# The order of two seven-step products and of the tiles beside them, in one transformer layer on one core

## The chip, the core and the metric

The kernel runs on one core of a Trainium2 chip. The metric is the time of one execution in microseconds (us), as the device gives it; several executions are made, and their median counts. TensorE multiplies, VectorE and ScalarE work on whole tiles of 128 partitions, POOL (GpSimd) and SP (SyncE) mostly issue transfers (DMAs). Each engine takes its own instructions in order and waits for others by semaphores.

## The reference

One decoder layer over 512 tokens of 1,024 channels. What matters here is the first part: a norm, one wide projection, and the two branches that are fed by it.

```python
u = _rmsnorm(h, norm1_g[l])
proj = u @ w_in[l]
a_glu, q, k, v, r, g_low, gate_a, gate_b = _split_cols(proj)

c = a_glu[..., :CONV_CH] * jax.nn.sigmoid(a_glu[..., CONV_CH:])
c = _causal_dwconv(c, conv_dw_w[l], conv_dw_b[l])
...
gk = jax.nn.log_sigmoid((g_low @ w_gate_up[l] + b_gate[l]).astype(jnp.float32)) / GATE_NORMALIZER
...
o = o.reshape(bsz, seq, GLA_VDIM).astype(x.dtype) * jax.nn.silu(r)
```

`v` (values) and `r` (out-gate) are 512 x 1,024 each. The depthwise convolution has 31 taps. Behind this come the attention, the merge, and a feed-forward part, which the change doesn't touch.

## The kernel before

**Splitting.** Every matrix product is made of three float32r products: each operand is split into a high part and a low part (`whi`, `wlo` for a weight), and `mm3` (line 378) adds low x high, high x low and high x high into one bank of PSUM. A weight tile is 128 x 1,024 (512 KB). `split_weight` (line 295) makes the high part with a cast on ScalarE and the low part in one of two ways: by a subtraction on VectorE, or, for the tiles named in `ADDED`, as a negated copy on ScalarE to which POOL adds the weight once more by a transfer (`wlo<-..., accum_op=ALU.add`).

**The order of weights.** `order` (line 168) lists all weight tiles by use. `load` (line 196) issues the transfer of the next of them on SP into one of four `raw` buffers; each split issues one further load. `weight` (line 348) hands out the next tile, sees that two more are split (`LOOK`), and lets `fill` issue a number (`RATES`) of small VectorE jobs from the `chains`: sums of the activations, and the convolution's taps (`conv_tap`). High and low parts have four buffers each. Instructions of one engine are ordered by a planner: it takes whatever is ready, earlier lines first; `issue_after` puts an instruction behind a given one of its engine.

**Seven steps.** `r` and `v` are made by a scheme with seven block products in place of eight (two of them, a11 and a12, are made at the start of the kernel, and a11's result is copied into the banks x by `opened`; five steps are left here: s1, n2, s4, n3, a22; `IN_STEPS`, line 56). Each step has two weight blocks (d = 0, 1) and two row groups (i = 0, 1), 24 matmuls. Weights and activations of a step are sums of quadrants. Those of the activations are made by `form` and `place` (lines 761 and 772) in the chains. Those of the weights are made by transfers that add (POOL): s1 is block (0,0) plus (0,1), in a `kept` tile; n2 is s1 plus (1,1), added in the same tile after s1 is split; s4 is block (1,1) as loaded; n3 is (0,1) plus (1,1); a22 is n2's tile plus (1,0). `load_block` (line 236), `add_n3` and `sum_on` (line 284) issue these.

**Banks.** `Inner` (line 953) runs the steps. n2, n3 and a22 add into the banks x, s1 and s4 into the banks y. After each step `sink` (line 983) takes the result, while the bank goes on adding: before, s1, n2 and a22 are copied on ScalarE, s4 is combined by VectorE from the bank, and n3 is copied by ScalarE to a `tmp` tile and subtracted by VectorE.

**Row layouts.** `w_r` lies in memory in columns. Its blocks are read from `rows_r`, which `lay_rows` (line 99) writes beforehand: eight tiles, two transfers each, from memory to memory, on SP.

**The stage.** After the start come convolution tiles (k = 0 to 4), each a gate tile and a value tile (`glu_gate`, `glu_value`, 24 matmuls each, weights `w_glu` 2k+1 and 2k), with two row layouts beside each of the first four; then all of w_r; the convolution tile 5; then s1 of w_v, the low-rank gate (`low_gate`, 16 matmuls), and the rest of w_v. The decay gate comes in three pieces (`gate`, line 937): small matmuls and absolute values, exponentials, logarithms; `GATE_AT` names the steps after which they are issued. Then the four heads, the first with the queries and keys `w_qk` 0 and 1.

```python
unit = Inner("w_r", sr)
unit.opened("x")
unit.run(IN_STEPS)
for k in range(GLU_AT[0], GLU_AT[0] + GLU_AT[1]):
    glu_gate(k)
    glu_value(k)
unit = Inner("w_v", vt)
unit.opened("x")
unit.run(IN_STEPS[:2])
glow = low_gate()
unit.run(IN_STEPS[2:], gate_at)
```

Of the kernel before, what the change touches and what calls it, by code (L numbers as in the profile page):

```python
# [10 lines left out]
F32 = mybir.dt.float32  # L11
# [31 lines left out]
ET = mybir.EngineType  # L43
ADDED = {("w_glu", 2 * k) for k in (2, 3, 4, 6, 7)} | {("w_qk", m) for m in range(2, KT)}
ADDED |= {(name, m) for name in ("w_gb", "w_gla") for m in range(KT)}
# [33 lines left out]
def trunk_layer(ctx: ExitStack, tc: tile.TileContext, a: dict, out: bass.AP):  # L79
# [113 lines left out]

    loaded = [None]

    def load():
        if len(raws) < len(order):
            name, j = order[len(raws)]
            if name in SEVEN:
                raws.append(load_block(name, *j))  # L200
                return
            raw = None
            if name == "w_up7":
                i, s = j
                name, j = "w_up", {"b": i, "x": FT + i}.get(s)
            if name == "w_r0":
                raw = raw_tile()
                for i in range(2):
                    c = slice((2 * j + i) * P, (2 * j + i + 1) * P)
                    dst = raw[:, i * T : (i + 1) * T].rearrange("p (c x) -> p c x", x=P)  # L210
                    loaded[0] = nc.sync.dma_start(dst, a["w_r"][:4, :, c].rearrange("c p x -> p c x"))
            elif j is not None:
                raw = raw_tile()
                loaded[0] = nc.sync.dma_start(raw, a[name.rstrip("0")][j])
            raws.append(raw)
# [11 lines left out]

    def keep_tile(name):
        if name != "w_down":
            return tp.tile([P, D], F32, tag="x", name=nm("kept"), bufs=3)  # L230
        return fp.tile([P, D], F32, tag="kept", name=nm("kept"), bufs=2)

    INNER = ("w_r", "w_v")
    LOADS = {"a11": (0, 0), "a12": (1, 0), "n2": (1, 1), "n3": (0, 1)}

    def load_block(name, pairs, step, d):

        first = "s1" if name in INNER else "a11"
        if step not in LOADS and step != first:
            return None  # L240
        src = block(name, pairs, d, *LOADS.get(step, (0, 0)))
        n = src.shape[-1]
        if step == first:
            dst = keep_tile(name)[:, :n]
# [10 lines left out]
        if step == "n2":  # L255
            kept[name, pairs, d, "b22"] = dst
        return dst
# [26 lines left out]
    def sum_on(name, pairs, step, d):  # L284

        where = {"a11": (0, 1), "n2": (1, 0)}
        if name in INNER:
            where["s1"] = (1, 1)
            if (step, d) in (("n2", 1), ("s4", 0)):
                add_n3(name, pairs, 0 if step == "n2" else 1)  # L290
        if step in where:
            nxt = block(name, pairs, d, *where[step])
            nc.gpsimd.dma_start(kept[name, pairs, d], nxt, accum_op=ALU.add)

    def split_weight(between=None):
        if len(ready) < len(order):
# [4 lines left out]
            if name in SEVEN or name == "w_up7":  # L301
                raw = operand(name, raw, *spec) if name in SEVEN else up_operand(raw, *spec)
                n = raw.shape[-1]
                if name == "w_up7" and spec[1] == "m":
                    both = wp.tile([P, D], F32R, tag="raw", name=nm("wm"), bufs=4)
                    nc.scalar.copy(both[:, :T], raw)
                    nc.vector.tensor_tensor(both[:, T:], raw, both[:, :T].bitcast(F32), ALU.subtract)
                    ready.append((both[:, :T], both[:, T:]))
                    load()
                    return  # L310
                hi = wp.tile([P, D], F32R, tag="whi", name=nm("whi"), bufs=4)[:, :n]
                lo = wp.tile([P, D], F32R, tag="wlo", name=nm("wlo"), bufs=4)[:, :n]
                nc.scalar.copy(hi, raw)  # L313
                pace[0] = nc.vector.tensor_tensor(lo, raw, hi.bitcast(F32), ALU.subtract)  # L314
# [275 lines left out]

    def sum_tile(i=0, dt=F32):
        if i == 0:
            return sp.tile([P, D], dt, tag="s", name=nm("f"))
        return tp.tile([P, D], dt, tag=("gain", "x")[i - 1], name=nm("sum"), bufs=(1, 3)[i - 1])

# [176 lines left out]
    def place(name, g):  # L772
        if name not in sums1:
            sums1[name] = [sum_tile(i, F32R) for i in {"n2": (1, 2)}.get(name, (0, 0))]
        hi, lo = (x[:, g * T : (g + 1) * T] for x in sums1[name])
        split_by(formed.pop((name, g)), hi, lo)
# [160 lines left out]
    def gate(piece):  # L937
        for h in range(HEADS):
# [10 lines left out]
            else:  # L949
                behind(lambda: nc.scalar.activation(ab[h], ab[h], AF.Ln, bias=1.0))  # L950
                nc.vector.tensor_tensor(ls[h], ls[h], ab[h], ALU.subtract)

    class Inner:
# [10 lines left out]
        def run(self, steps, at=lambda step, i: None):  # L964
            steps = list(steps)
            while steps:
                step, d = steps.pop(0)
                steps.pop(0)
                parts = [(d, weight(self.name, (IN_PAIRS, step, d))) for d in (0, 1)]
                for i in range(2):  # L970
# [3 lines left out]
                    for d, w in parts:  # L974
                        for j in range(2):
# [3 lines left out]
                            mm3(acc, (ah, al), (w[0][:, c], w[1][:, c]), opens, d == 1 and j == 1, step != "s1")  # L979
                    self.sink(step, i, acc)  # L980
                    at(step, i)

        def sink(self, step, i, acc):
            res = self.res
            at = {"n2": (i, 1), "s4": (i, 1), "s1": (2 + i, 1), "n3": (2 + i, 1), "a22": (2 + i, 0), "a12": (i, 0)}
            key = at[step]
            if step in ("a12", "n2", "s1", "a22"):
                res[key] = heap()
                nc.scalar.copy(res[key], acc)
            elif step == "n3":  # L990
                y = tmp()
                nc.scalar.copy(y, acc)
                nc.vector.tensor_tensor(res[key], res[key], y, ALU.subtract)
            else:
                nc.vector.tensor_tensor(res[key], acc, res[key], ALU.subtract)

    def quadrant(step, p):
        k0, k1 = IN_PAIRS[p]
        if step in ("a12", "a22"):
            lo = T // 2 if step == "a22" else 0  # L1000
            return tuple(x[:, lo : lo + T // 2] for x in acts1[k1])
        return tuple(x[:, p * T // 2 : (p + 1) * T // 2] for x in sums1[step])

# [15 lines left out]
    sums_scope.close()  # L1019
# [687 lines left out]
```

## Time and profile before

| what | value |
|---|---|
| runs | 834.89, 833.38, 833.07 us; median 833.38 us |
| the profiled execution | 837.78 us, its span 836.1 us, mean granted clock 0.992 |
| matmuls | 4,090 |
| moved by DMA | 135.60 MB, mean 162 GB/s |

The profile is one execution. A row of the timeline has the start and the duration in us, the engine, the line, the operation, what it writes and reads, how many were merged (x), and in brackets how long the engine had been idle before it and who released it. A row of the windows has the stretch, and for each engine (TensorE, its weight loads, VectorE, ScalarE, POOL) the busy time and the number of instructions; then TensorE's granted clock as a share of full speed, the busy share of the DMA engines, and GB/s. Matmuls overlap, so their own durations (0.39 us) are longer than the distance from one to the next; what counts is the distance. "DMA to landing" is the time from the issue of a transfer to its end: least, median, most. "x4" behind a line's name counts its instructions, and three numbers with slashes are least, median and most in ns. The names `f`, `sum` and `s` are activation sums; in w_r, `f` belongs to s1, s4 and n3 and `sum` to n2.

### The profile page before, as it was taken

The numbers are of one execution on the slowest core, as the hardware profiler recorded it, in microseconds if no ns is written. First come the engines' busy times: TensorE is split into PE (matmuls) and PEld (weight loads), VectorE is DVE, ScalarE is ACT, GpSimd is POOL, SyncE is SP. The second block draws the span as 40 slices with busy tenths as digits, with TensorE's granted clock in tenths as the row PEclk, the third lists the DMA queues.
The fourth block names the chain that finished last, engine by engine and source line by source line (L and its number), as shares of the span: only waits on it lengthen the run. The fifth ranks groups of instructions, "written<-read, shape, count | busy, mean of one in ns | idle before, by whom it ended". The sixth has DMA issues, their size and how long they took to land.

```text
span 836.1 us, 11021 instructions
## 1 busy us (share of the span) xinstructions
PE 819.6 (98%) x4090; PEld 694.7 (83%) x4090; DVE 677.2 (81%) x996; ACT 471.5 (56%) x671; POOL 116.8 (14%) x139
## 2 busy tenths in 40 slices
PE   9999899999999999999999999999999999999996
PEld 7888688788888888888888898888789888988885
DVE  6899598899999889854678768769957788588896
ACT  7673346795534553359445559655446643577554
POOL 2001202011211221000001012111112012220111
PEclk9999899999999999999999999999999999999999
DMA  9499878658666677321346639456825737556562
GB/s 316 149 271 295 156 217 184 170 154 211 143 147 151 151 175 186 119 100 51 126 99 194 175 137 227 102 126 151 223 92 151 176 77 226 151 152 192 137 125 101
DMA packets 49925, 135.60 MB, mean 162 GB/s; under 512 B 4592, under 2 KB 17152, under 8 KB 49872
## 3 DMA queue, kind: packets, MB, share of 16 engines
q1 hardware_dynamic: 37456, 90.91, 30.9%
q0 software_dynamic: 12240, 43.78, 29.4%
q8 instruction: 32, 0.52, 0.2%
q10 hardware_dynamic: 176, 0.20, 0.1%
q14 instruction: 21, 0.17, 0.1%
HBM read 132.79 MB, written 6.29 MB: 166 GB/s over the span
## 4 chain that ended last, share of the span: by engine, by line
PE 79%; DVE 8%; DMA 7%; ACT 3%; issue 2%; POOL 0%; POOLq 0%; ACTq 0%; DVEq 0%; SPq 0%
PE mm L383 22%; PE mm L384 22%; PE mm L382 22%; PE ax L382 2%; PE mm L652 2%; PE ax L383 2%; PE ax L384 2%; DMA kept<-in_w_o_dram 2%; DVE c L799 2%; DMA kept<-in_w_v_dram 1%; DMA raw<-rows 1%; DVE wlo L314 1%; DVE wlo L339 1%; DMA kept<-rows 1%; PE ax L1125 1%
## 5 line engine op out<-in xcount | busy, mean ns | idle before, releaser
L382 PE MATMUL mm<-uh,wlo 128*128 128x512 f32 (+1 forms) x636 | 237.1, 373 | 0.0
L383 PE MATMUL mm<-ul,whi 128*128 128x512 f32 (+1 forms) x636 | 234.9, 369 | 0.6 <-DVE ul L473 0.6
L384 PE MATMUL mm<-uh,whi 128*128 128x512 f32 (+1 forms) x636 | 234.4, 369 | 0.0
L799 DVE SCALAR_TENSOR_TENSOR c<-h,pp,c 128x507 f32<-128x507 f32 (+21 forms) x240 | 169.7, 731 | 2.9
L384 PEld LDWEIGHTS mm<-uh,whi 128*128 128x128 f32 x636 | 119.8, 188 | 20.4
L383 PEld LDWEIGHTS mm<-ul,whi 128*128 128x128 f32 x636 | 120.0, 189 | 19.2 <-DVE ul L473 1.1
L382 PEld LDWEIGHTS mm<-uh,wlo 128*128 128x128 f32 x636 | 119.9, 189 | 18.3
L330 ACT CAST whi<-raw 128x1024 fp32r<-128x1024 f32 x94 | 97.4, 1042 | 35.2 <-PE mm L384 28.5
L332 ACT ACTIVATE wlo<-raw 128x1024 fp32r<-128x1024 f32 x45 | 47.5, 1059 | 74.2 <-PE mm L382 72.4
L313 ACT CAST whi<-raw 128x1024 fp32r<-128x1024 f32 (+1 forms) x53 | 53.9, 1027 | 49.9 <-PE mm L384 36.4
L313 ACT CAST whi<-kept 128x1024 fp32r<-128x1024 f32 (+1 forms) x44 | 44.3, 1010 | 54.9 <-DMA kept<-rows 16.8
L1366 DVE SCALAR_TENSOR_TENSOR tmp<-mm,pp,tmp 128x511 f32<-128x511 f32 (+1 forms) x88 | 64.5, 742 | 12.6 <-ACT tmp L1364 12.2
L314 DVE TENSOR_TENSOR wlo<-raw,whi 128x1024 fp32r<-128x1024 f32 (+1 forms) x53 | 65.7, 1248 | 9.0 <-ACT whi L313 8.5
L339 DVE TENSOR_TENSOR wlo<-raw,whi 128x1024 fp32r<-128x1024 f32 x49 | 59.3, 1219 | 13.0 <-ACT whi L330 12.6
L314 DVE TENSOR_TENSOR wlo<-kept,whi 128x1024 fp32r<-128x1024 f32 (+1 forms) x44 | 51.3, 1172 | 20.4 <-ACT whi L313 20.2
L1364 ACT ACTIVATE tmp<-mm,pp 128x512 f32<-128x512 f32 x44 | 33.3, 775 | 11.6 <-PE mm L384 11.6
L1286 DVE TENSOR_TENSOR hres<-hres,mm 128x512 f32<-128x512 f32 (+1 forms) x49 | 32.4, 670 | 2.4 <-PE mm L384 2.3
L333 POOL DMA_DIRECT2D wlo<-in_w_up_dram x18 | 15.5, 862 | 95.6 <-ACT wlo L332 77.7
L383 PE MATMUL mm<-wlo,sh 128*128 128x512 f32 x66 | 25.9, 393 | 0.0
L384 PE MATMUL mm<-whi,sh 128*128 128x512 f32 x66 | 25.7, 389 | 0.0
L382 PE MATMUL mm<-h,wlo 128*128 128x512 f32 x64 | 25.4, 397 | 0.0
L382 PE MATMUL mm<-whi,sl 128*128 128x512 f32 x66 | 25.1, 391 | 0.2 <-ACT whi L313 0.2
(362 smaller groups left out, 1645.3 us busy)
## 6 DMA issues: line engine op xcount, KB each, us to landing
raw<-in_w_up_dram SPq DMA_DIRECT2D x44, 512.0 KB, 4.2
wlo<-in_w_up_dram POOLq DMA_DIRECT2D x18, 512.0 KB, 7.5
raw<-in_w_glu_dram SPq DMA_DIRECT2D x16, 512.0 KB, 4.5
raw<-in_w_down_dram SPq DMA_DIRECT2D x15, 512.0 KB, 5.0
kept<-in_w_down_dram POOLq DMA_DIRECT2D x10, 512.0 KB, 5.2
raw<-in_w_v_dram SPq DMA_DIRECT2D x8, 512.0 KB, 6.5
rows<-in_w_r_dram SPq DMA_DIRECT2D x16, 256.0 KB, 7.2
raw<-in_w_qk_dram SPq DMA_DIRECT2D x8, 512.0 KB, 6.0
```

The source lines that it names most:

```text
L313: nc.scalar.copy(hi, raw)
L314: pace[0] = nc.vector.tensor_tensor(lo, raw, hi.bitcast(F32), ALU.subtract)
L330: nc.scalar.copy(hi, raw)
L332: pace[0] = nc.scalar.activation(lo, raw, AF.Copy, scale=-1.0)
L339: pace[0] = nc.vector.tensor_tensor(lo, raw, hi.bitcast(F32), ALU.subtract)
L382: nc.tensor.matmul(acc, ll, rh, start=first, stop=False, **kw)
L383: nc.tensor.matmul(acc, lh, rl, start=False, stop=False, **kw)
L384: nc.tensor.matmul(acc, lh, rh, start=False, stop=last, **kw)
L799: nc.vector.scalar_tensor_tensor(y[:, s:], c[:, : T - s], w, y[:, s:], ALU.mult, ALU.add)
L1286: nc.vector.tensor_tensor(hres[t, n][:, c], hres[t, n][:, c], x[:, c], op)
L1364: nc.scalar.activation(z, acc, AF.Identity, bias=pp[:, PP_FB + m : PP_FB + m + 1], scale=w[2])
L1366: nc.vector.scalar_tensor_tensor(z[:, s:], acc[:, : T - s], w[j], z[:, s:], ALU.mult, ALU.add)
```

## The change

- The steps run in the order s1, s4, n2, n3, a22. The s4 block (1,1) is the one that is loaded; n2 is split without a load of its own, and such steps no longer use up a load (`skipped`, and `load` calls itself).
- Four convolution tiles come before w_r. The tiles 4 and 5 are put into w_r and w_v: the gate tile behind s1 (in w_v behind the low-rank gate), the value tile behind n3. The banks x are opened after the gate tile.
- s1, s4 and a22 are copied by ScalarE; n2 and n3 are subtracted by VectorE straight from the bank.
- All 16 row layouts are issued beside the tiles 0 and 1, after the first and after the second `w_glu` load.
- `w_qk` 0 and 1 get their low parts by adding transfers. Three of the four subtractions of the log decays go to POOL.
- In `Inner` the taps are issued after each half step, behind its `sink`, no longer before its matmuls. The sums of n2 go to four convolution buffers; the second `kept` tile of w_v goes to the buffer `gain`, the first has a third `x` buffer.
- The decay gate's pieces come after s4, n2 and n3 of w_v (i = 1 each).

```diff
-ADDED = {("w_glu", 2 * k) for k in (2, 3, 4, 6, 7)} | {("w_qk", m) for m in range(2, KT)}
+ADDED = {("w_glu", 2 * k) for k in (2, 3, 4, 6, 7)} | {("w_qk", m) for m in range(0, KT)}
-IN_STEPS = [(step, d) for step in ("s1", "n2", "s4", "n3", "a22") for d in (0, 1)]
-GLU_AT = (5, 1, 2)
+IN_STEPS = [(step, d) for step in ("s1", "s4", "n2", "n3", "a22") for d in (0, 1)]
+GLU_AT = (4, 2, 2)
-GATE_AT = [("n2", 0), ("s4", 0), ("n3", 1)]
+GATE_AT = [("s4", 1), ("n2", 1), ("n3", 1)]
...
-    order += [("w_r", (IN_PAIRS, step, d)) for step, d in IN_STEPS]
-    order += [("w_glu", 2 * k + j) for k in range(GLU_AT[0], late) for j in (1, 0)]
-    v_steps = [("w_v", (IN_PAIRS, step, d)) for step, d in IN_STEPS]
-    order += v_steps[:2] + [("w_low", 0), ("w_low", 1)] + v_steps[2:]
+    for i, name in enumerate(("w_r", "w_v")):
+        for step, d in IN_STEPS:
+            order.append((name, (IN_PAIRS, step, d)))
+            if (step, d) == ("s1", 1):
+                order += [("w_low", 0), ("w_low", 1)] if name == "w_v" else []
+                order.append(("w_glu", 2 * (GLU_AT[0] + i) + 1))
+            if (step, d) == ("n3", 1):
+                order.append(("w_glu", 2 * (GLU_AT[0] + i)))
...
                 raws.append(load_block(name, *j))
+                if name in INNER and raws[-1] is None:
+                    load()
                 return
...
-                loaded[0] = nc.sync.dma_start(raw, a[name.rstrip("0")][j])
+                sent[name, j] = nc.sync.dma_start(raw, a[name.rstrip("0")][j])
...
-    def keep_tile(name):
+    def keep_tile(name, d):
+        if name == "w_v" and d == 1:
+            return tp.tile([P, D], F32, tag="gain", name=nm("kept"), bufs=1)
...
+    IN_LOADS = {"s1": (0, 0), "s4": (1, 1), "n3": (0, 1)}
...
-            if (step, d) in (("n2", 1), ("s4", 0)):
-                add_n3(name, pairs, 0 if step == "n2" else 1)
+            if (step, d) in (("s4", 0), ("s4", 1)):
+                add_n3(name, pairs, d)
...
+                skipped = name in INNER and raws[len(ready)] is None
                 ready.append((hi, lo))
-                load()
+                if not skipped:
+                    load()
...
-    def weight(name, j, ahead=LOOK):
+    def weight(name, j, ahead=LOOK, taps=True):
...
-        fill(RATES.get(name if name != "w_glu" or j < 2 * (KT - GLU_AT[2]) else "late", RATE))
+        if taps:
+            fill(RATES.get(name if name != "w_glu" or j < 2 * (KT - GLU_AT[2]) else "late", RATE))
...
+        if name == "n2":
+            sums1[name, g] = [ctile(F32R) for _ in range(2)]
...
-        for n in ("s1", "n2", "s4", "n3"):
+        for n in ("s1", "s4", "n2", "n3"):
             chain += [(1, lambda n=n, g=g: place(n, g)) for g in range(2)]
...
-        for j in range(2 * k, min(2 * k + 2, KT)):
-            with tc.issue_after(loaded[0].ins):
-                lay_rows(j)
+        if k < 2:
+            for j in ((0, 4, 1, 5), (6, 7, 2, 3))[k]:
+                with tc.issue_after(sent["w_glu", 1 - k].ins):
+                    lay_rows(j)
...
-                nc.vector.tensor_tensor(ls[h], ls[h], ab[h], ALU.subtract)
+                (nc.gpsimd if h >= 1 else nc.vector).tensor_tensor(ls[h], ls[h], ab[h], ALU.subtract)
...
-                parts = [(d, weight(self.name, (IN_PAIRS, step, d))) for d in (0, 1)]
+                parts = [(d, weight(self.name, (IN_PAIRS, step, d), taps=False)) for d in (0, 1)]
...
                     self.sink(step, i, acc)
+                    fill(RATES[self.name])
...
-            if step in ("a12", "n2", "s1", "a22"):
+            if step in ("a12", "s4", "s1", "a22"):
                 res[key] = heap()
                 nc.scalar.copy(res[key], acc)
-            elif step == "n3":
-                y = tmp()
-                nc.scalar.copy(y, acc)
-                nc.vector.tensor_tensor(res[key], res[key], y, ALU.subtract)
             else:
-                nc.vector.tensor_tensor(res[key], acc, res[key], ALU.subtract)
+                nc.vector.tensor_tensor(res[key], res[key], acc, ALU.subtract)
...
-    unit = Inner("w_r", sr)
-    unit.opened("x")
-    unit.run(IN_STEPS)
-    for k in range(GLU_AT[0], GLU_AT[0] + GLU_AT[1]):
-        glu_gate(k)
-        glu_value(k)
-    unit = Inner("w_v", vt)
-    unit.opened("x")
-    unit.run(IN_STEPS[:2])
-    glow = low_gate()
-    unit.run(IN_STEPS[2:], gate_at)
+    for i, (name, res) in enumerate((("w_r", sr), ("w_v", vt))):
+        unit = Inner(name, res)
+        unit.run(IN_STEPS[:2])
+        if name == "w_v":
+            glow = low_gate()
+        glu_gate(GLU_AT[0] + i)
+        unit.opened("x")
+        at = gate_at if name == "w_v" else lambda step, i: None
+        unit.run(IN_STEPS[2:8], at)
+        glu_value(GLU_AT[0] + i)
+        unit.run(IN_STEPS[8:], at)
```

More of the change, by code (lines that the diff above doesn't have):

```diff
@@ L192, in trunk_layer @@
     pace = [None]
-    loaded = [None]
+    sent = {}
     def load():
@@ L210, in load @@
                     dst = raw[:, i * T : (i + 1) * T].rearrange("p (c x) -> p c x", x=P)
-                    loaded[0] = nc.sync.dma_start(dst, a["w_r"][:4, :, c].rearrange("c p x -> p c x"))
+                    nc.sync.dma_start(dst, a["w_r"][:4, :, c].rearrange("c p x -> p c x"))
             elif j is not None:
                 raw = raw_tile()
-                loaded[0] = nc.sync.dma_start(raw, a[name.rstrip("0")][j])
+                sent[name, j] = nc.sync.dma_start(raw, a[name.rstrip("0")][j])
             raws.append(raw)
@@ L234, in trunk_layer @@
     LOADS = {"a11": (0, 0), "a12": (1, 0), "n2": (1, 1), "n3": (0, 1)}
+    IN_LOADS = {"s1": (0, 0), "s4": (1, 1), "n3": (0, 1)}
     def load_block(name, pairs, step, d):
         first = "s1" if name in INNER else "a11"
-        if step not in LOADS and step != first:
+        loads = IN_LOADS if name in INNER else LOADS
+        if step not in loads:
             return None
-        src = block(name, pairs, d, *LOADS.get(step, (0, 0)))
+        src = block(name, pairs, d, *loads[step])
         n = src.shape[-1]
         if step == first:
-            dst = keep_tile(name)[:, :n]
+            dst = keep_tile(name, d)[:, :n]
             kept[name, pairs, d] = dst
@@ L254, in load_block @@
                 add_n3(name, pairs, d)
-        if step == "n2":
+        if step == ("s4" if name in INNER else "n2"):
             kept[name, pairs, d, "b22"] = dst
@@ L589, in trunk_layer, with sum_tile @@
     sums_scope, sp = scoped("sums", 6, "right")
[L591 to L594, printed above, removed]
+    def sum_tile(dt=F32):
+        return sp.tile([P, D], dt, tag="s", name=nm("f"))
     whole = {}
@@ L772, in place @@
     def place(name, g):
[L773 to L776, printed above, removed]
+        if name == "n2":
+            sums1[name, g] = [ctile(F32R) for _ in range(2)]
+        elif g == 0:
+            both = [sum_tile(F32R) for _ in range(2)]
+            for n in range(2):
+                sums1[name, n] = [x[:, n * T : (n + 1) * T] for x in both]
+        split_by(formed.pop((name, g)), *sums1[name, g])
     def sums_chain():
@@ L1001, in quadrant @@
             return tuple(x[:, lo : lo + T // 2] for x in acts1[k1])
-        return tuple(x[:, p * T // 2 : (p + 1) * T // 2] for x in sums1[step])
+        return tuple(x[:, p % 2 * T // 2 : (p % 2 + 1) * T // 2] for x in sums1[step, p // 2])
     def gate_at(step, i):
```

## The prediction

> **What bounds the kernel now.** I read the page first, then the busy time by stretches, then the order of TensorE's matmuls around the two gaps, and last what the other engines and queues did there.
>
> ```profile
> span 836.1 us, 11021 instructions
> PE 819.6 (98%) x4090; PEld 694.7 (83%) x4090; DVE 677.2 (81%) x996; ACT 471.5 (56%) x671; POOL 116.8 (14%) x139
> ...
> 100.00:105.00 5.00, 4.59 (x11) 3.63 (x12) 5.00 (x7) 2.10 (x4) 0.85 (x1) 0.50 1.00 179
> ...
> 160.00:165.00 5.00, 2.95 (x10) 2.02 (x9) 3.37 (x6) 4.99 (x9) 0.00 (x0) 0.81 0.02 5
> ...
> 170.00:420.00 250.00, 250.00 (x1169) 209.01 (x1168) 208.33 (x333) 136.23 (x193) 30.48 (x33) 1.00 0.55 143
> ```
>
> TensorE is the bound: busy 98% of the span, and 250 of 250 us behind the changed stage. VectorE has 208 of those 250, so an earlier start of TensorE is passed on to the end. Only its idle time and its slow clock can be won, and in the stage that the diff touches there are two such places: 94 to 105 us, and 160 to 166 us, each with idle time and a granted clock of 0.5 to 0.8 behind it.
>
> ```profile
> 88.78 0.39 PE L382 MATMUL mm<-whi,f 128*128 128x512 f32 x1
> ...
> 94.00 0.39 PE L384 MATMUL mm<-whi,f 128*128 128x512 f32 x1
> ...
> 106.57 0.39 PE L382 MATMUL mm<-whi,f 128*128 128x512 f32 x1
> ...
> 160.16 0.39 PE L384 MATMUL mm<-whi,f 128*128 128x512 f32 x1
> 162.60 0.50 PE L382 MATMUL mm<-whi,ul 128*128 128x512 f32 x1 [2.05 <-ACT tmp L992]
> ...
> 169.80 0.39 PE L382 MATMUL mm<-uh,wlo 128*128 128x512 f32 x1
> ```
>
> The first two rows are the first and the last of the 24 matmuls of step s1 of w_r: (94.00 - 88.78) / 23 = 0.227 us from start to start. A step of 24 is 5.45 us, a convolution tile (48) 10.9.
> - Step n2 of w_r could start at 94.23 and step s4 starts at 106.57: 12.34 us for 5.45 of work, a loss of **6.89**.
> - Step a22 of w_v could start at 160.39 and the first query starts at 169.80: 9.41 for 5.45, a loss of **3.96**, of which 162.60 - 160.39 = 2.21 is the gap and 1.75 the slow clock behind it.
>
> ```profile
> 76.30 1.23 DVE L314 TENSOR_TENSOR wlo<-kept,whi 128x1024 fp32r<-128x1024 f32 x1 [1.68 <-ACT whi L313]
> ...
> 81.94 1.22 DVE L314 TENSOR_TENSOR wlo<-kept,whi 128x1024 fp32r<-128x1024 f32 x1
> ...
> 84.73 0.87 POOL L260 DMA_DIRECT2D raw<-rows  x1 [12.57 <-DVE c L799]
> ...
> 86.54 1.18 POOL L293 DMA_DIRECT2D kept<-rows  x1
> 90.36 0.87 POOL L293 DMA_DIRECT2D kept<-rows  x1 [2.65 <-issue]
> ...
> 95.03 1.04 ACT L313 CAST whi<-kept 128x1024 fp32r<-128x1024 f32 x1 [10.40 <-DMA kept<-rows]
> 97.60 1.05 ACT L313 CAST whi<-kept 128x1024 fp32r<-128x1024 f32 x1 [1.53 <-DMA kept<-rows]
> ...
> 159.11 1.28 ACT L950 ACT_TABLE_LOAD   x1
> 160.41 1.67 ACT L950 ACTIVATE tmp<-tmp 128x512 f32<-128x512 f32 x3
> 161.98 0.56 ACT L992 COPY tmp<-mm 128x512 f32<-128x512 f32 x1
> ```
>
> The first loss: n2's weights are s1's with one more block added by a transfer, which may start only when s1's low part is made (77.5 and 83.2). The transfers are issued at 86.54 and 90.36, since POOL's queue first sat 12.57 us in front of another add, and ScalarE can cast their results at 95.03 and 97.60. The second: the copy of n3's result (L992), which a22 needs gone from its bank, stands behind a table load and three logarithms on ScalarE.
>
> **The change, part by part.**
>
> *Reordering w_r and w_v* (s1, a gate tile, s4, n2, n3, a value tile, a22). Matmuls, transfers and their sizes stay the same in number. Between s1 and n2 there are now a tile of 5.45 and s4 of 5.45: n2 starts 16.35 after s1's start instead of 5.45. Once issued, the two adds needed 95.03 - 86.54 = 8.5 and 97.60 - 90.36 = 7.2. That fits, so the 6.89 goes. In w_v, n3 is subtracted by VectorE straight from the bank, with no copy on ScalarE, and the value tile gives it 5.45 before a22: the 3.96 goes. Together **-10.85**. What is late next follows.
>
> *The value tile of w_r* takes w_glu 8, which is in ADDED both before and after (its low part is a negated copy plus an adding transfer). In the plain run of tiles its buffers came free two tiles, 10.9 us, ahead of use. Now four whi buffers reach back to n2's first half, whose last use is the 18th of 24 matmuls: 6 x 0.227 + 5.45 (n3) = 6.8 us.
>
> ```profile
> 55.89 1.06 ACT L332 ACTIVATE wlo<-raw 128x1024 fp32r<-128x1024 f32 x1 [1.23 <-PE mm L382]
> ...
> 57.26 0.87 POOL L333 DMA_DIRECT2D wlo<-in_w_glu_dram  x1 [9.62 <-ACT wlo L332]
> ...
> DMA to landing us min/median/max: 3.6/5.7/13.5
> ...
> DMA to landing us min/median/max: 5.1/7.0/12.0
> ...
> 562.20 0.38 PE L382 MATMUL ax<-n,wlo 128*128 128x256 f32 x1 [1.56 <-ACT mm L1554]
> ...
> 562.30:566.00 3.70, 3.70 (x28) 3.57 (x29) 3.67 (x7) 2.39 (x4) 0.00 (x0) 1.00 0.73 267
> ```
>
> High part 1.04 (as the cast at 95.03), low part 1.06, then 57.26 - 56.95 = 0.31 to the issue: 2.4. The two lines of landings are those of the adds into kept (L293) and into wlo (L333). With 3.6 the chain is 6.0 and nothing waits; with 5.7 it is 8.1, 1.3 late; with 7.0 it is 9.4, 2.6 late; with 12.0, 7.6 late. I take 5.7, as L293's adds are the ones in this stage: **+1.3**. A gap of 1.56 at 562 us left the clock at 1.00, so I add no slow clock.
>
> By the Trainium skill (TensorE: Matmul & The Clock Gate, "HAM oscillation") only gaps over about 3.4 us throttle TensorE. The gap of 2.05 at 160 us was followed by a granted clock of 0.81, so here the measurement decides; by the rule a gap of 2.6 would cost 1.75 less than I charge for it below.
>
> *n2 and n3 now follow each other in the same two banks*; before, s4 lay between. n3's first half may start when VectorE has taken n2's first half, 2.72 us after its end. The nearest rows are s4's subtractions.
>
> ```profile
> 110.69 0.68 DVE L995 TENSOR_TENSOR h<-mm,h 128x512 f32<-128x512 f32 x1
> ...
> 154.66 1.28 DVE L995 TENSOR_TENSOR h<-mm,h 128x512 f32<-128x512 f32 x2
> ...
> L946 DVE TENSOR_SCALAR h<-ax,pp x3: 740/740/750, 148.5 to 149.8; 128x512 f32<-128x512 f32 x3
> ```
>
> In w_r: s4's first half ended at 106.57 + 2.72 = 109.29 and was taken at 111.37, 0.64 before the limit. In w_v: s4 ran from 160.39 - 10.9 = 149.49, its first half ended at 152.21 and was taken at 155.34, 3.13 later, 0.4 past the limit. I take **+0.4**; the bounds are 0 and, if two splits (1.22 each) and four gate operations (0.74) go ahead in VectorE's queue, 5.4 + 0.68 - 2.72 = 3.4.
>
> *First query and key by adding transfers*: two VectorE operations of 1.22 go, two of 1.06 on ScalarE, two POOL issues and 2 x 512 KB come. The query's buffers come free with n3's end, and the value tile and a22 cover 10.9; the chain is 2.4 + 7.0 = 9.4: 0. Without the cover: were the table load and logarithms (1.28 + 4 x 0.56 = 3.5) to stand ahead, it is 2.0 late. Three subtractions of the log decays move from VectorE to POOL; the key's add may queue behind them, but the heads that need them come a head later. 0, at most one such wait of 2.0.
>
> *Row layouts earlier*: all 16 issues are moved up SP's queue, from behind the eighth and the tenth convolution load to behind the first (8) and the second (8).
>
> ```profile
> 19.06 24.94 SPq L214 DMA_DIRECT2D raw<-in_w_glu_dram  x8
> 44.05 8.05 SPq L105 DMA_DIRECT2D rows<-in_w_r_dram  x8
> ...
> 25.00:30.00 5.00, 5.00 (x24) 4.14 (x23) 3.80 (x5) 3.84 (x5) 0.00 (x0) 1.00 0.43 150
> ...
> DMA to landing us min/median/max: 3.1/4.2/6.9
> ...
> 31.71 2.35 DVE L339 TENSOR_TENSOR wlo<-raw,whi 128x1024 fp32r<-128x1024 f32 x2
> ...
> 38.58 1.29 DVE L556 TENSOR_TENSOR ul<-f,uh 128x512 fp32r<-128x512 f32 x2
> ...
> 39.47 0.40 PE L382 MATMUL mm<-uh,wlo 128*128 128x256 f32 x2
> ...
> 41.28 2.36 DVE L339 TENSOR_TENSOR wlo<-raw,whi 128x1024 fp32r<-128x1024 f32 x2
> ...
> L105 SPq DMA_DIRECT2D rows<-in_w_r_dram x16: 564/728/2736, 44.1 to 65.6; - x16
> ...
> DMA to landing us min/median/max: 5.6/7.2/9.4
> ```
>
> The DMA engines are at 0.43 there, so there is room. Behind eight issues (8.05) the second load leaves at 19.4 + 8.05 = 27.4; at the median 4.2 (the first line of landings) it lands at 31.6 and is split by 33.9, before the 34.06 at which its low part was ready: 0, with 2.55 as the upper bound (first rival below). The taps' new place, the sums in other buffers and w_v's kept tile in the gain buffer hide behind TensorE's matmuls: 0.
>
> **Sum**: -10.85 + 1.3 + 0.4 = **-9.15**. The profiled execution took 837.78 (span 836.1 and 1.7 around it), so 828.6; it is 4.4 above the median of the runs, 833.38, and I carry that over: **824.2**.
>
> **The rivals.**
> 1. *The second convolution load lands late.* At 6.9 it lands at 34.3, is split at 36.6 instead of 34.06, and VectorE does everything behind it 2.55 later. TensorE has nothing to give there: its matmuls at 39.5 follow the low parts that VectorE ends at 39.87 with no slack. Loss 2.55 + 1.75 of slow clock: 828.5. Against it: the share of 0.43. By the Trainium skill (DMA: Bandwidth & Descriptors, "Queues, rings and completion order") each DMA engine takes a ring's descriptors in order, which speaks for it.
> 2. *The add into w_glu 8 takes the 7.0 of the other wlo adds*: 2.6 idle, long enough for the slow clock (the gap of 2.05 was), 1.75: 824.2 + 3.05 = 827.3.
> 3. *The change doesn't remove the first loss.* From low part to cast it was 95.03 - 77.53 = 17.5 in all, queueing included. If s1's second weight is split only just before use (1.36 into s1), 16.35 - 1.36 - 2.3 = 12.7 are there: 4.8 late, + 1.75: 830.7. Against it: the adds that held POOL's queue now come after s4's splits.
> 4. *Slower: the layouts crowd out the convolution loads.* Before, 16 layouts with their company took from 44.05 to 65.6 + 9.4 (the last line), 31 us. Taking that from 19.4, the second load lands half way, at 34.9 (split at 37.2, 3.1 late), and w_glu 3, behind all of them, at 50.4 (split at 52.7, where the second tile starts at 88.78 - 4 x 10.9 = 45.2: 7.5 late). With two slow clocks 14.1: 824.2 + 14.1 = 838.3. It decides once w_glu 3 lands after about 45.4. For it: SP's order is free to put all 16 first. Against it: blocks of w_r and convolution tiles were loaded in those 31 us as well.
>
> **How the numbers follow.** Forecast 0.45 (its own range 822.5, with no new wait, to 826), rival 1 0.13, rival 2 0.20, rival 3 0.12, rival 4 0.10. The range 821.8 to 831.5 holds all but rival 4 and the long ends of the rest. A measurement of this kernel can tell some 0.2%, 1.7 us: faster 0.85, within 0.06 (ends of rivals 3 and 4), slower 0.09.
>
> **What would show it.** Right: no idle time of TensorE before n2 of w_r and a22 of w_v, clock 1.0 there, the casts of kept no longer waiting for a transfer; about 1 us of idle before the value tile of w_r, put down to the add into wlo; n3's first matmul waiting at most half a us for VectorE. Wrong: TensorE idle between 33 and 46 us, or over 2 us before that value tile or the first query.

## The result, and the profile after

The kernel after the change took 829.45 us (median of 4 runs, 828.47 to 830.39), the kernel before 833.89 on the same chip (833.07 to 834.89): a ratio of 0.9939, interval 0.9914 to 0.9964, or 4.4 us less. The profiled execution took 828.47 against 837.78.

The page of the profile after (span and engines), two stretches around the place of the first loss, and TensorE's two longest kinds of wait (line waited at, what ended the wait, total us, times, longest):

```profile
span 826.8 us, 11023 instructions
PE 813.3 (98%) x4090; PEld 689.9 (83%) x4090; DVE 676.8 (82%) x991; ACT 471.0 (57%) x669; POOL 123.1 (15%) x144
...
100.00:105.00 5.00, 4.70 (x21) 3.57 (x19) 4.94 (x8) 1.98 (x3) 0.04 (x1) 1.00 0.91 202
105.00:110.00 5.00, 3.62 (x16) 3.00 (x17) 5.00 (x8) 0.78 (x1) 0.00 (x0) 1.00 0.06 17
...
PE mm L395 <- DMA wlo<-in_w_glu_dram: 1.9, 2, 1.7
PE mm L395 <- DMA wlo<-in_w_qk_dram: 1.6, 1, 1.6
```

The two old losses are no longer there: n2 follows without a wait, TensorE is busy 5.00 of 5.00 us from 155 to 160, where w_v's a22 now runs, and the clock is 1.00 in both stretches. Two new waits are there, each for a low part made by an adding transfer. ScalarE's low part of w_glu 8 and POOL's issue of its add, then TensorE's matmuls around the two waits:

```profile
97.71 1.06 ACT L344 ACTIVATE wlo<-raw 128x1024 fp32r<-128x1024 f32 x1 [1.80 <-PE mm L396]
...
99.18 0.87 POOL L345 DMA_DIRECT2D wlo<-in_w_glu_dram  x1 [6.67 <-ACT wlo L344]
...
104.31 0.39 PE L397 MATMUL mm<-whi,f 128*128 128x512 f32 x1
106.38 0.50 PE L395 MATMUL mm<-uh,wlo 128*128 128x512 f32 x1 [1.69 <-DMA wlo<-in_w_glu_dram]
...
181.58 0.39 PE L397 MATMUL mm<-uh,whi 128*128 128x512 f32 x1
183.56 0.50 PE L395 MATMUL mm<-uh,wlo 128*128 128x512 f32 x1 [1.60 <-DMA wlo<-in_w_qk_dram]
```

The first is w_r's value tile, waiting for the add into w_glu 8: 106.38 - 104.31 - 0.23 = 1.84 lost. The second is the second head's query, waiting for w_qk 2: 1.75 lost. So of the two profiled executions: -6.89 - 3.96 + 1.84 + 1.75 = -7.26. The remaining 2.05 of the 9.31 lies outside the changed stage. Some 1.0 of it comes ahead of the stage (the matmul that starts at 33.72 before starts at 32.69), and most of the rest is the wait of 1.56 at 562 us, which the prediction quotes and which has no counterpart in this execution.

POOL's adds into a block of n3 (`raw`) and into s1's tiles (`kept`), and the first of n2's casts, which had waited for a transfer before:

```profile
71.01 0.85 POOL L270 DMA_DIRECT2D raw<-rows  x1 [5.30 <-DMA raw<-rows]
71.67 1.10 POOL L303 DMA_DIRECT2D kept<-rows  x1
74.22 0.86 POOL L303 DMA_DIRECT2D kept<-rows  x1 [1.45 <-DVE c L813]
...
84.13 1.05 ACT L323 CAST whi<-kept 128x1024 fp32r<-128x1024 f32 x1
```

The adds leave at 71.67 and 74.22 instead of 86.54 and 90.36; the casts at 84.13 and 88.91 wait for no transfer. That agrees with the reordering, but the adds' *issue* is 15 to 16 us earlier. Most of that is w_r's own start, a tile earlier (s1's first matmul comes at 77.34 instead of 88.78); a longer way from s1 to n2 gives none of the rest. It made me doubt the cause.

### The profile page after: what moved, and what is told of

Its sections match the earlier page's. It is cut to its first block, busy times and chain, and to the rows that moved or that the text cites. A ratio compares the mean times of both kernels' runs of the same rounds, so it can differ in the third digit from the quotient of the medians.

```text
span 826.8 us, 11023 instructions
## 1 busy us (share of the span) xinstructions
PE 813.3 (98%) x4090; PEld 689.9 (83%) x4090; DVE 676.8 (82%) x991; ACT 471.0 (57%) x669; POOL 123.1 (15%) x144
## 4 chain that ended last, share of the span: by engine, by line
PE 78%; DVE 11%; DMA 4%; issue 3%; ACT 2%; POOL 1%; SPq 0%; POOLq 0%; ACTq 0%; DVEq 0%
PE mm L396 22%; PE mm L395 22%; PE mm L397 22%; DVE c L813 4%; PE ax L395 2%; DMA wlo<-in_w_glu_dram 2%; PE mm L663 2%; PE ax L396 2%; PE ax L397 2%; DVE wlo L324 1%; DMA kept<-rows 1%; DMA x<-in_x_dram 1%; PE ax L1137 1%; DVE tmp L1378 1%; PE ax L474 0%
## 5 line engine op out<-in xcount | busy, mean ns | idle before, releaser
L813 DVE SCALAR_TENSOR_TENSOR c<-h,pp,c 128x507 f32<-128x507 f32 (+20 forms) x240 | 169.9, 733 | 2.8
L344 ACT ACTIVATE wlo<-raw 128x1024 fp32r<-128x1024 f32 x47 | 49.5, 1058 | 69.6 <-PE mm L395 65.5
L351 DVE TENSOR_TENSOR wlo<-raw,whi 128x1024 fp32r<-128x1024 f32 x47 | 56.9, 1220 | 16.7 <-ACT whi L342 16.3
```

The lines of the kernel that those rows point to most:

```text
L344: pace[0] = nc.scalar.activation(lo, raw, AF.Copy, scale=-1.0)
L813: nc.vector.scalar_tensor_tensor(y[:, s:], c[:, : T - s], w, y[:, s:], ALU.mult, ALU.add)
```

## The experiments

A median here is of the kernel's runs beside runs of the kernel before on the same chip; those of one group share chip and runs.

**First group: the edits priced at nothing and the new wait** (before: 834.6 us).

*The kernel after again, unchanged.*

> The changed kernel once more. Theory A (the profiled execution of the kernel before was an unusually long one, the changed kernel's was an ordinary one): the profile again shows the waits of TensorE for the adds into w_glu 8 and w_qk 2 at 1.5 to 2.5 us each, no loss before n2 and a22, total 828 to 830 us. Theory B (the changed kernel has new waits that come in some executions only): the profile shows losses of 2 us or more at other places, and the total moves by more than 2 us from 829.5.

831.68 us (12 runs, 828.72 to 835.36), ratio 0.9968 (0.9952 to 0.9984). This profiled execution took 834.58. Its matmuls at the value tile, then two stretches (the last three numbers are the clock, the DMA share and GB/s):

```profile
108.93 0.80 PE L395 MATMUL mm<-uh,wlo 128*128 128x512 f32 x1 [3.58 <-DMA wlo<-in_w_glu_dram]
...
105.00:110.00 5.00, 1.43 (x5) 0.88 (x4) 5.00 (x8) 1.13 (x2) 0.00 (x0) 0.77 0.26 70
110.00:115.00 5.00, 5.00 (x14) 3.92 (x13) 1.19 (x2) 0.00 (x0) 0.00 (x0) 0.54 0.00 0
```

The wait for w_glu 8 is 3.58 here, with a slow clock behind it: the prediction's second rival, in another execution of the same kernel. Neither theory holds whole: the places of the waits are A's, the size of this one and the total are B's.

*w_glu 8's low part by VectorE instead of the adding transfer.*

```diff
-ADDED = {("w_glu", 2 * k) for k in (2, 3, 4, 6, 7)} | {("w_qk", m) for m in range(0, KT)}
+ADDED = {("w_glu", 2 * k) for k in (2, 3, 6, 7)} | {("w_qk", m) for m in range(0, KT)}
```

> The low part of w_glu 8 is made by VectorE again, all else as in the changed kernel. If the wait before the value tile of w_r (1.96 us in the profile) is the add's chain of 2.4 us plus the transfer against the 6.8 us that the buffers leave, it goes and the kernel is 1.5 to 2 us shorter, about 827.5 us. Rival: VectorE, 5.0 of 5.0 us busy there, takes 1.2 us more and is late with the next subtraction from the banks or the next split: no gain, or under 0.5 us.

829.01 us (6 runs), 0.994 (0.9922 to 0.9957): 2.7 less than the kernel after in the same group. The wait at the value tile is gone, the one for w_qk 2 (1.4) stays. By the medians the add's price is 2.7 us on this chip, wait and clock together; the size is rough, since the intervals of the two kernels just meet.

*All log-decay subtractions on VectorE, as before.*

```diff
-                (nc.gpsimd if h >= 1 else nc.vector).tensor_tensor(ls[h], ls[h], ab[h], ALU.subtract)
+                nc.vector.tensor_tensor(ls[h], ls[h], ab[h], ALU.subtract)
```

> All four subtractions of the log decays on VectorE, all else as in the changed kernel. Theory: the three on POOL (1.56 us each) slow VectorE's operations beside them (1.79 and 2.32 us where 0.68 and 1.22 are usual), so VectorE gains nothing; without them the first head's scan comes at most 1 us later or earlier, the operations of VectorE go back to 0.68 and 1.22 us, and the wait for the add into w_qk 2 (1.9 us) shrinks by 0 to 1.5 us. Rival: VectorE has 2.05 us more to do, the scan is 2 us later, and the wait grows to 3 to 4 us.

831.7 us (12 runs), 0.9976 (0.9961 to 0.9991): the same as the kernel after, so no worth of the move to POOL can be seen. What it does to VectorE is told at the end.

*First query and key's low parts by VectorE, as before.*

```diff
-ADDED = {("w_glu", 2 * k) for k in (2, 3, 4, 6, 7)} | {("w_qk", m) for m in range(0, KT)}
+ADDED = {("w_glu", 2 * k) for k in (2, 3, 4, 6, 7)} | {("w_qk", m) for m in range(2, KT)}
```

> The first query's and key's low parts by VectorE again, all else as in the changed kernel. My prediction put this edit at 0: within 0.7 us of the changed kernel. Rival: VectorE, which has no idle time there, gets two operations of 1.2 us more, the first head's scan and with it ScalarE's exponentials and the low part of w_qk 2 come 2 us later, and TensorE's wait there grows from 1.9 to about 4 us.

831.67 us (12 runs), 0.9971 (0.9953 to 0.9989): the edit costs and brings nothing that can be seen. TensorE's one long wait at the first query in this kernel:

```profile
160.80 0.50 PE L395 MATMUL mm<-uh,wlo 128*128 128x512 f32 x1 [1.19 <-DVE wlo L351]
```

With two more splits VectorE is late at the first query instead, while the wait at w_qk 2 goes: one wait is exchanged for another.

**Second group: which part removes the losses** (before: 834.37 us).

*The kernel before again, unchanged.*

> The kernel before once more, with a profile of its own. Theory A: this execution is an ordinary one near 834 us; the loss before n2 of w_r is smaller than the 6.89 us of the first profile, or has no slow clock behind it, and the mean granted clock is above 0.992; the two losses add up to some 6 to 7 us. Theory B: the two losses are again 10.5 to 11 us and the profile is about 838 us, so that profiling itself adds some 4 us to this kernel and none to the changed one.

833.41 us (12 runs), 0.9992 (0.9976 to 1.0008); profiled execution 832.54. Around the first loss, then the stretch of the second, and ScalarE ahead of it; below, the row of the first profile of before in which the second of these casts stands:

```profile
93.03 0.39 PE L384 MATMUL mm<-whi,f 128*128 128x512 f32 x1
94.32 0.50 PE L382 MATMUL mm<-whi,sum 128*128 128x512 f32 x1 [0.90 <-ACT whi L313]
95.58 0.50 PE L383 MATMUL mm<-wlo,sum 128*128 128x512 f32 x1 [0.76 <-DVE wlo L314]
98.38 0.49 PE L382 MATMUL mm<-whi,sum 128*128 128x512 f32 x1 [1.39 <-ACT whi L313]
99.64 0.50 PE L383 MATMUL mm<-wlo,sum 128*128 128x512 f32 x1 [0.77 <-DVE wlo L314]
...
105.24 0.39 PE L382 MATMUL mm<-whi,f 128*128 128x512 f32 x1
...
155.00:170.00 15.00, 15.00 (x68) 12.40 (x67) 14.26 (x22) 13.12 (x19) 0.00 (x0) 1.00 0.30 103
...
153.39 1.99 ACT L313 CAST whi<-kept 128x1024 fp32r<-128x1024 f32 x2
```

```profile
158.04 1.05 ACT L313 CAST whi<-kept 128x1024 fp32r<-128x1024 f32 x1 [2.32 <-DMA kept<-in_w_v_dram]
```

The first loss is there again: 105.24 - 93.26 - 5.45 = 6.53. The second is not: TensorE is busy 15.00 of 15.00 us at clock 1.00. In the first profile the cast at 158.04 had waited 2.32 us for a late transfer, and the table load, the logarithms and the copy behind it were late with it. Here both casts are done by 155.38. This is theory A.

*The kernel before with the early row layouts alone.*

```diff
-        for j in range(2 * k, min(2 * k + 2, KT)):
-            with tc.issue_after(loaded[0].ins):
-                lay_rows(j)
+        if k < 2:
+            for j in ((0, 4, 1, 5), (6, 7, 2, 3))[k]:
+                with tc.issue_after(sent["w_glu", 1 - k].ins):
+                    lay_rows(j)
```

> The kernel before with the row layouts alone moved up to the first two convolution tiles, the order of the steps as before. If the first loss came from the late layouts (POOL's queue stood 12.6 us in front of an add whose block had not landed), n2's weights are ready when s1 ends and most of the first loss goes: 3 to 6 us shorter than before. Rival (mine in the prediction): the order of the steps is what does it; the adds still take 7 to 8.5 us from issue against a step of 5.45 us, so at most half of the loss goes, 0 to 3 us.

826.51 us (6 runs), 0.9918 (0.989 to 0.9947). SP's queue and POOL's, one low part of s1, the first cast of n2, and two stretches; below them SP's row of before for the same loads, and the same two stretches of the kernel before, run again:

```profile
19.44 3.40 SPq L105 DMA_DIRECT2D rows<-in_w_r_dram  x3
...
55.80 13.28 SPq L249 DMA_DIRECT2D raw<-rows  x4
...
74.53 1.22 DVE L315 TENSOR_TENSOR wlo<-kept,whi 128x1024 fp32r<-128x1024 f32 x1
...
76.62 0.86 POOL L261 DMA_DIRECT2D raw<-rows  x1 [5.11 <-issue]
77.22 1.18 POOL L294 DMA_DIRECT2D kept<-rows  x1
81.78 0.87 POOL L294 DMA_DIRECT2D kept<-rows  x1 [3.38 <-DVE wlo L315]
...
84.61 1.05 ACT L314 CAST whi<-kept 128x1024 fp32r<-128x1024 f32 x1
...
20.00:45.00 25.00, 25.00 (x162) 22.70 (x161) 20.67 (x29) 17.20 (x24) 1.45 (x2) 1.00 1.00 307
...
90.00:110.00 20.00, 20.00 (x90) 16.57 (x89) 17.88 (x23) 9.72 (x13) 0.86 (x1) 1.00 0.66 178
```

```profile
71.27 2.86 SPq L248 DMA_DIRECT2D raw<-rows  x4
```

```profile
20.00:45.00 25.00, 25.00 (x163) 22.69 (x162) 21.13 (x30) 17.46 (x25) 1.02 (x2) 1.00 0.47 159
...
90.00:110.00 20.00, 16.19 (x61) 12.12 (x60) 14.76 (x19) 8.59 (x11) 1.73 (x2) 0.91 0.80 182
```

With s1 and n2 still side by side, TensorE is busy 20.00 of 20.00 us. The layouts leave from 19.44 on, into DMA engines that had been at 0.47; the blocks laid out by rows are asked for from 55.80 instead of 71.27. In the kernel before, a block that was asked for from 71.27 on took a median of 11.0 us to land, which fits the add into n3's block that POOL could issue only at 84.73, though that row names a VectorE operation. Here the like add leaves at 76.62 after 5.11 us of standing, and s1's adds behind it at 77.22 and 81.78, 1.5 and 0.4 us after their low parts are made (75.75 and 81.38). The first cast of n2 is 10.4 us earlier (84.61 against 95.03). This part alone removes the first loss. The gain of 7.9 us is above the 3 to 6 that I expected; the two profiled executions, 825.77 here and 832.54 of the kernel before run again, differ by 6.77, near the loss of 6.53.

*The kernel after with the row layouts late, as before.*

```diff
-        if k < 2:
-            for j in ((0, 4, 1, 5), (6, 7, 2, 3))[k]:
-                with tc.issue_after(sent["w_glu", 1 - k].ins):
-                    lay_rows(j)
+        for j in ((0, 4), (1, 5), (6, 7), (2, 3))[k]:
+            with tc.issue_after(loaded[0].ins):
+                lay_rows(j)
```

> The changed kernel with the row layouts issued beside the first four convolution tiles as before (two each, in the new order of tiles). Mine: the order of the steps gives n2 16.3 us behind s1's start, so n2 still doesn't wait; but w_r starts a tile earlier, and its first blocks come 10 us later than in the changed kernel, so s1 may wait: 0 to 4 us longer than the changed kernel. Rival: the early layouts are what removed the loss: 5 us or more longer, near the time before.

837.06 us (8 runs), 1.0036 (1.0021 to 1.0051): longer than before by 2.7 us, as the rival says. The rows of POOL, ScalarE and VectorE, and among them TensorE's first matmul of n2 (whose sums are named `c` in this kernel), its first of n3 and its first of the value tile:

```profile
84.39 0.85 POOL L270 DMA_DIRECT2D raw<-rows  x1 [11.57 <-DMA raw<-rows]
85.01 1.15 POOL L303 DMA_DIRECT2D kept<-rows  x1
...
94.75 0.39 PE L395 MATMUL mm<-whi,c 128*128 128x512 f32 x1
...
95.73 1.04 ACT L323 CAST whi<-kept 128x1024 fp32r<-128x1024 f32 x1 [5.62 <-DMA kept<-rows]
...
102.42 1.04 ACT L323 CAST whi<-raw 128x1024 fp32r<-128x1024 f32 x1 [3.73 <-DMA raw<-rows]
...
103.50 1.23 DVE L324 TENSOR_TENSOR wlo<-raw,whi 128x1024 fp32r<-128x1024 f32 x1 [1.75 <-ACT whi L323]
...
105.29 0.68 DVE L1006 TENSOR_TENSOR h<-h,mm 128x512 f32<-128x512 f32 x1
...
106.12 0.62 PE L395 MATMUL mm<-whi,f 128*128 128x512 f32 x1 [3.89 <-DVE h L1006]
...
113.58 0.50 PE L395 MATMUL mm<-uh,wlo 128*128 128x512 f32 x1 [0.16 <-DMA wlo<-in_w_glu_dram]
```

The change without the early layouts keeps POOL's queue standing (11.57 us, here plainly for a load of raw from rows), the add behind it leaves at 85.01, and n2's second cast comes at 95.73. n3's block is later still; its split stands in VectorE's queue ahead of the subtraction that should empty n2's bank, and TensorE waits 3.9 us for that bank. From n2's start to the value tile's TensorE needs 113.58 - 94.75 = 18.83 us for 10.9 of work, a loss of 7.9. Only 1.9 of it falls in n2 (its last matmul starts at 101.85, and 101.85 + 0.23 - 94.75 - 5.45 = 1.88): the longer way from s1 helps n2 much as predicted, but the loss comes back one step later, at n3, whose block is late by the same layouts. This run takes one part out of the bundle; the reordering by itself was not run.

*The kernel before with n3 subtracted by VectorE from the bank, without ScalarE's copy.*

```diff
-                y = tmp()
-                nc.scalar.copy(y, acc)
-                nc.vector.tensor_tensor(res[key], res[key], y, ALU.subtract)
+                nc.vector.tensor_tensor(res[key], res[key], acc, ALU.subtract)
```

> The kernel before with n3 subtracted by VectorE straight from the bank, with no copy on ScalarE; nothing else changed. If the second loss (3.96 us with its slow clock) is the copy behind the logarithms, it goes: 2.5 to 4 us shorter than before. Rival: a22's first matmul then waits for VectorE or for its own weights instead, and less than 1 us is won.

834.24 us (12 runs), 0.9999 (0.9985 to 1.0013): no gain. The copy that the prediction blamed for the second loss costs nothing that the medians show; what it would save in an execution with a late landing wasn't seen.

**Third group: what holds the kernel after back** (before: 834.15 us).

*The kernel after, with w_glu 8 and w_qk 2 both split by VectorE.*

```diff
-ADDED = {("w_glu", 2 * k) for k in (2, 3, 4, 6, 7)} | {("w_qk", m) for m in range(0, KT)}
+ADDED = {("w_glu", 2 * k) for k in (2, 3, 6, 7)} | {("w_qk", m) for m in (0, 1, 3, 4, 5, 6, 7)}
```

> The changed kernel with the low parts of w_glu 8 and w_qk 2 made by VectorE. Theory: beside the early layouts, the rest of the change only adds the two waits for adding transfers (1.7 to 3.6 us with w_glu 8, 1.2 to 1.6 us with w_qk 2, and a slow clock behind the longer ones); without them it is as fast as the kernel before with early layouts, ratio 0.990 to 0.993, and no wait of TensorE above 0.7 us between 45 and 190 us. Rival: VectorE, with 2.4 us more to do where it has no idle time, is late for the query or the scan: a new wait of 1 to 2 us, ratio 0.994 to 0.996.

829.58 us (10 runs), 0.9945 (0.9925 to 0.9965). The matmul at TensorE's longest wait in this kernel:

```profile
212.99 1.16 PE L1156 MATMUL ax<-ident,o 128*128 128x128 f32 x6 [1.47 <-DVE o L1150]
```

That is the rival's range. The waits for w_glu 8 and w_qk 2 are gone, but VectorE, given two more splits, is late with the first head's output at 213 us; it is busy 28.51 of the 30 us from 185 to 215. A wait of 0.73 at 61.99 is for the add into an earlier convolution tile. From 45 to 215 us TensorE is idle 3.1 us here and 0.45 in the kernel before with the early layouts alone: 2.7 of the 3.6 us between the two profiled executions.

*The early row layouts alone, again, and with the tiles in plain order* (0 to 3, then 4 to 7):

```diff
-            for j in ((0, 4, 1, 5), (6, 7, 2, 3))[k]:
+            for j in range(4 * k, 4 * k + 4):
```

> The kernel before with the early layouts alone, once more, beside the others on one chip: ratio 0.990 to 0.993 if the first measurement (0.9918, its interval 0.989 to 0.9947) holds; TensorE without a wait between 45 and 125 us. Rival: the first measurement was a lucky one, and the ratio is 0.995 or more.

> The kernel before with early layouts, laid in their natural order (0 to 3 beside the first tile, 4 to 7 beside the second) and not in the order of use (0, 4, 1, 5, then 6, 7, 2, 3). Theory: what matters is that all of them are through before w_r's first blocks are split at 73 us, so the order is worth under 1 us: ratio within 0.0015 of the other one. Rival: s1's blocks 4 and 5 come 4 to 6 us later, the adds in POOL's queue are late again, and 2 to 4 us of the first loss come back.

826.86 us (6 runs), 0.9914 (0.988 to 0.9948), and 826.17 us (6 runs), 0.9896 (0.9868 to 0.9924). The gain repeats on another chip; the two orders of the layouts are 0.7 us apart, within the spread of the runs. In both, TensorE is busy 80.00 of 80.00 us from 45 to 125. The last is the fastest version found: the kernel before with 16 transfers issued earlier, 3.4 us less than the kernel after with both its waits cured.

## Why the prediction came out as it did

The direction held and 829.45 lies in the range, but the forecast of 824.2 is 5.25 too low, the same kernel took 831.68 on another chip, just past the end of the range at 831.5, and two steps behind the forecast failed.

- **"That fits, so the 6.89 goes", put down to the reordering.** The loss went, but the early layouts alone are enough for that: they take 7.3 to 8.0 us off (826.51 against 834.37, 826.17 against 834.15); the rest of the change without them adds 2.7 (837.06 against 834.37), for there the longer way from s1 cuts n2's loss to 1.9 and n3 loses the rest. The prediction set "Row layouts earlier" at 0, "with 2.55 as the upper bound", and so saw only a risk in them. The answer was in a row that it quoted: POOL's issue at 84.73 behind 12.57 us of standing, with s1's add next in the queue at 86.54. The sum gave the add more time after its issue and took the standing as given, instead of asking what POOL stood for and when that was sent. Rival 3 did count the standing, and was held unlikely because "the adds that held POOL's queue now come after s4's splits". They don't: in the kernel after, too, such an add (71.01) leaves right before s1's first (71.67), and with late layouts (84.39) right before s1's second (85.01).
- **The second loss, 3.96.** It belonged to one execution. The kernel before, profiled again, hasn't got it, and the edit that should cure it alone gives 0.9999. It needed a late landing; with the casts on time, the same order of ScalarE's work costs nothing.
- **"it is 4.4 above the median of the runs, 833.38, and I carry that over".** The profiled execution was long because it held that loss, the longer wait at 562 and a start later by 1.0 (s1 of w_r at 88.78, and at 87.81 in the second profile of the same kernel). Taking the loss out as a gain of the change and then the whole 4.4 as well counts the loss twice against the median. The profiles differ by 9.31, where the sum says 9.15; that is luck, for the 2.05 from outside the stage makes up for the two waits that cost more than the sum has. The medians differ by 4.4. With the first loss as measured again and the two new waits, 833.4 - 6.5 + 1.84 + 1.75 = 830.5, between the two medians of the kernel after, 829.45 and 831.68.
- **The value tile of w_r, +1.3.** The mechanism was right and the term too small: 1.84 in one profile, 3.58 of wait and a slow clock in the other, 2.7 in the medians of the group. The low part starts at 97.71, 104.54 - 97.71 = 6.83 ahead of use, as predicted; but the high part isn't ahead of it, so 1.47 to the issue and not 2.4, and the add then takes 7.2 us to land (9.1 in the second profile) and not the 5.7 that were taken from the adds into kept. 1.47 + 7.2 - 6.83 = 1.84. Rival 2, with 7.0, had the better figure.
- **n2 and n3 in the same banks, +0.4.** 0 in the kernel after, 0.4 (in w_v) in the one with both adds cured. But with late layouts this wait is the largest, 3.9, beyond the bound of 3.4: there the split ahead of the subtraction itself waits for a landing.
- **First query and key, 0; log decays, 0.** Both agree in time, each undone alone, but not for the reasons given: the first is one wait exchanged for another, and the second a gain on VectorE that is lost again beside POOL.
- **Not foreseen: w_qk 2, +1.75.** The prediction looked at the first head's adds alone. POOL's issue of w_qk 2's add, merged with the next, in the kernel after:

```profile
175.62 1.82 POOL L345 DMA_DIRECT2D wlo<-in_w_qk_dram  x2 [14.64 <-DVE c L813]
```

  w_qk 2's add leaves at 175.62, and TensorE wants it at 181.58 + 0.23 = 181.81, only 6.2 us later; the prediction's own figure for such a transfer is 7.0, and here it takes 7.9. Why it leaves no earlier stays open; its row names a tap on VectorE.
- **Rivals 1, 3 and 4** didn't occur. The layouts went out in small lots between the convolution loads, so the second load stood behind three of them, not eight or sixteen (in the kernel after, three layouts leave from 18.94 on and the second load at 22.39).

Left open: the kernel after costs some 2 to 6 us against the early layouts alone, by their ratios to the kernel before (0.9939 and 0.9968 against 0.9896 to 0.9918); the two weren't run side by side. The wait for w_glu 8 is about 2.7 of it in one group. With both adds cured TensorE still has waits up to 213 us; that VectorE's load is their cause is argued from the one at L1150 and wasn't tried by itself. Nor was the reordering tried together with the early layouts and nothing else.

## What to carry to other kernels

When an operand is late, follow each transfer that feeds it back to its issue, and ask what every queue on that way was standing for; a transfer that can be sent earlier, into DMA engines with room (0.47 here), may be worth the whole loss, so price a moved transfer as a gain too. Take a loss from a second execution before counting it, and don't add the profiled execution's excess over the median to a sum that already removes part of that excess. Run the parts of a bundle one at a time: here one part brings more than the whole, and the rest, with the reordering that looked like the cure, costs time.

## What the hardware showed that I had not expected

**VectorE slows beside POOL.** The log-decay subtractions on POOL in the kernel after, VectorE's work in the same microseconds, and the same subtractions all on VectorE in the kernel that undoes the move (ns minimum, median, maximum):

```profile
149.34 4.69 POOL L966 TENSOR_TENSOR h<-h,tmp 128x512 f32<-128x512 f32 x3 [12.25 <-ACT tmp L965]
...
149.40 0.68 DVE L1007 TENSOR_TENSOR h<-h,mm 128x512 f32<-128x512 f32 x1
150.00 1.17 DVE L813 SCALAR_TENSOR_TENSOR c<-h,pp,c 128x485 f32<-128x485 f32 x1
151.09 1.79 DVE L966 TENSOR_TENSOR h<-h,tmp 128x512 f32<-128x512 f32 x1
152.80 2.32 DVE L324 TENSOR_TENSOR wlo<-kept,whi 128x1024 fp32r<-128x1024 f32 x1
```

```profile
L966 DVE TENSOR_TENSOR h<-h,tmp x4: 684/686/690, 151.0 to 152.8; 128x512 f32<-128x512 f32 x4
```

One such subtraction takes VectorE 0.69 us alone and 1.79 beside POOL's, a split 2.32 instead of 1.22, and the tap at 150.00 1.17 instead of 0.72. Three operations of 0.69 were moved away, and 1.10 + 1.10 + 0.45 = 2.65 us came back. From that tap's start to the split's end VectorE needs 155.12 - 150.00 = 5.12 us here and 4.26 with all four subtractions of its own, so the move saves it nothing. VectorE's subtraction at 149.40, which reads a PSUM bank, kept its 0.68. The Trainium skill (GPSIMD Engine Reference, "1. Specifications") says that POOL's SBUF interfaces are shared with VectorE and contended by VectorE's instructions with two SBUF inputs; the trace agrees: the subtraction and the split, with two SBUF inputs each, are slowed, the one with a PSUM input isn't.

**Idle time and the clock.** Gaps of 1.69 and 1.60 us left the clock at 1.00; one of 3.58 was followed by 0.77 and 0.54. By the Trainium skill (TensorE: Matmul & The Clock Gate, "HAM oscillation") only gaps over about 3.4 us throttle, which fits these three. It doesn't fit the first profile of before, where the one gap of 2.05 was followed by 0.50 from 164 to 166 us, nor the kernel before run again, where four waits of 0.76 to 1.39 within 6 us were followed by 0.50 from 102 to 104; that several short waits add up is a guess that no run here tested.
